# Head-wise top-1 routing: the routing logits move into the experts' matmuls, and half of the masking moves to GpSimd

## The chip, the cores and the metric

The kernel runs on one core of one Trainium2 chip. The metric is the device time of one launch in microseconds (us): 1763.26 us is the median of two runs of the kernel before (1754.2 and 1772.32 us). All data are float32.

## What is computed

```
route_logits = x @ route_w                       # x: 64 x 1024 tokens of 1024, route_w: 1024 x 16
best_head    = argmax(route_logits, axis=-1)     # one of 16 heads per token
x_heads      = x.reshape(B, S, 16, 64)
for h in range(16):
    out[:, :, h, :] = (x_heads[:, :, h, :] @ experts[h]) * (best_head == h)[:, :, None]
```

There are 65536 tokens, 512 tiles of 128 tokens. All sixteen 64x64 products are formed for every token, and all but one head of a token's output are then set to zero by the mask. 268 MB are read and 268 MB written.

## The kernel before, in words

A tile is 128 tokens on the 128 partitions by 1024 columns (512 KB). Four tiles make a group; `for g in range(NG + 1)` goes over 128 groups, and inside it `for t in range(T)` over a group's four tiles. The loop is software-pipelined by one group: while group g is transposed, group g-1 goes through the experts.

Per tile, TensorE makes eight 128x128 transposes (line 99) into the PSUM tile `ps_t`, four to a bank, and ScalarE copies each half to the SBUF tile `xt` (line 102), so that the contraction index lies on the partitions. `expert_tile` then issues 32 small matmuls (line 141): the array is used as four 64x64 tiles, `half` choosing the upper or lower 64 partitions (an even or an odd head) and `th` the upper or lower 64 tokens. Here `xt` is the stationary operand and the expert's 64x64 matrix in `ew` the moving one. VectorE evacuates all 1024 columns of `ps_e` with one multiplication by the mask (line 146) into `ot`.

Once per group, `route` computes the logits separately: eight matmuls with `route_w` stationary and 512 tokens moving (line 111), a ScalarE copy (line 115), four transposes back (line 118), a VectorE reduction over four column groups (line 120) and five small VectorE instructions on 128x64 elements that make the mask (lines 124 to 132).

In the trace every float32 matmul of the code is two MATMUL instructions, each with a weight load (LDWEIGHTS) of its own: 32 in the code are 64 and 64 there. Transposes are one and one. Loads of `x` (line 88) and stores of the output (line 163) are both issued on SyncE's queue, SP, in program order. Twenty `xin` buffers let the loads run 20 tiles ahead: a load waits until the transposes of the tile 20 before it are done. A store waits for the masking of its tile. The order on each engine follows the program.

## Time and profile before

| | |
|---|---|
| median of the two runs | 1763.26 us |
| the profiled execution | 1754.08 us, its span 1752.3 us |
| mean granted TensorE clock | 0.962 |
| busy share of the span | TensorE matmuls 87%, weight loads 65%, VectorE 47%, ScalarE 36%, GpSimd 0% |
| DMA queue of loads and stores | 536.94 MB, 86.8% of 16 engines' time |
| DMA queue of instructions | 310 packets, 5.08 MB, 1.2% |
| median time to landing | load 5.8 us, store 6.5 us |

The shares are of the whole span. A line of the costliest groups gives busy time and mean length of one instruction, and behind the second bar the idle time of the engine before such instructions with what ended it. Matmuls overlap in the array, so the mean length of one is not the distance from one to the next; that distance is read from the timeline. "Issue" is time in which an engine waited for nothing that the profile shows.

### The profile page before, as it was taken

The numbers are of one execution on the slowest core, as the hardware profiler recorded it, in microseconds if no ns is written. First come the engines' busy times: TensorE is split into PE (matmuls) and PEld (weight loads), VectorE is DVE, ScalarE is ACT, GpSimd is POOL, SyncE is SP. The second block draws the span as 40 slices with busy tenths as digits, with TensorE's granted clock in tenths as the row PEclk, the third lists the DMA queues.
The fourth block names the chain that finished last, engine by engine and source line by source line (L and its number), as shares of the span: only waits on it lengthen the run. The fifth ranks groups of instructions, "written<-read, shape, count | busy, mean of one in ns | idle before, by whom it ended". The sixth has DMA issues, their size and how long they took to land.

```text
span 1752.3 us, 84634 instructions
## 1 busy us (share of the span) xinstructions
PE 1517.8 (87%) x39424; PEld 1132.8 (65%) x39424; DVE 824.7 (47%) x1282; ACT 638.2 (36%) x1153; POOL 0.8 (0%) x7
## 2 busy tenths in 40 slices
PE   7888889888889988988889898888888888888898
PEld 5666666666666666666666676666666666665666
DVE  2444444444445544444444454445444444454455
ACT  3333333333333333333333333333333333333343
POOL 0000000000000000000000000000000000000000
PEclk8999999999999999899999999999999999999999
DMA  8999888998889989898998888989998889998864
GB/s 307 379 347 321 297 309 305 320 329 301 306 293 325 328 293 327 283 326 313 315 318 299 315 307 300 312 303 336 312 321 307 313 312 322 314 319 297 300 262 195
DMA packets 149903, 542.68 MB, mean 310 GB/s; under 512 B 18480, under 2 KB 18480, under 8 KB 149552
## 3 DMA queue, kind: packets, MB, share of 16 engines
q1 hardware_dynamic: 147456, 536.94, 86.8%
q8 instruction: 310, 5.08, 1.2%
q10 hardware_dynamic: 2096, 0.33, 0.1%
q14 instruction: 41, 0.34, 0.1%
HBM read 268.76 MB, written 268.44 MB: 307 GB/s over the span
## 4 chain that ended last, share of the span: by engine, by line
PE 86%; issue 12%; DMA 1%; DVE 0%; ACT 0%; ACTq 0%
PE ps_e L141 35%; PE ps_t L99 31%; PE ps_r L111 15%; PE ps_l L118 4%; DMA ew<-in_experts_dram 1%; DVE ot L146 0%; ACT lgt L115 0%; ACTq L70 0%; ACT xt L102 0%; ACTq L115 0%
## 5 line engine op out<-in xcount | busy, mean ns | idle before, releaser
L146 DVE TENSOR_TENSOR ot<-ps_e,mask 128x1024 f32<-128x1024 f32 x512 | 627.0, 1225 | 556.6 <-PE ps_e L141 543.5
L102 ACT COPY xt<-ps_t 128x512 f32<-128x512 f32 x1024 | 565.2, 588 | 662.8 <-PE ps_t L99 662.2
L141 PE MATMUL ps_e<-ew,xt 64*64 64x64 f32 x32768 | 658.0, 226 | 159.9 <-issue 155.2
L141 PEld LDWEIGHTS ps_e<-ew,xt 64*64 64x64 f32 x32768 | 566.8, 138 | 271.6 <-issue 263.3
L99 PE MATMUL ps_t<-ident,xin 128*128 128x128 f32 x4096 | 604.2, 286 | 42.5 <-issue 36.9
L99 PEld LDWEIGHTS ps_t<-ident,xin 128*128 128x128 f32 x4096 | 458.3, 144 | 186.7 <-issue 159.6
L111 PE MATMUL ps_r<-xt,rw 128*32 128x512 f32 x2048 | 279.2, 642 | 20.8 <-issue 20.8
L115 ACT COPY lgt<-ps_r 128x512 f32<-128x512 f32 x128 | 74.9, 585 | 435.3 <-PE ps_r L111 435.3
L120 DVE TENSOR_REDUCE lg<-ps_l 128x64 f32<-128x256 f32 x128 | 54.4, 425 | 342.5 <-PE ps_l L118 342.5
L111 PEld LDWEIGHTS ps_r<-xt,rw 128*32 128x32 f32 x2048 | 57.1, 114 | 127.2 <-issue 117.3
L118 PE MATMUL ps_l<-ident,lgt 128*128 128x128 f32 x512 | 84.0, 286 | 4.3 <-issue 3.8
L118 PEld LDWEIGHTS ps_l<-ident,lgt 128*128 128x128 f32 x512 | 54.8, 142 | 27.0 <-ACT lgt L115 22.8
L126 DVE TENSOR_TENSOR hit<-lg,mx 128x64 f32<-128x64 f32 x128 | 28.9, 225 | 4.4
L132 DVE TENSOR_TENSOR mask<-hit,top 128x64 f32<-128x64 f32 x128 | 28.8, 225 | 4.4
L128 DVE TENSOR_TENSOR hit<-hit,rank 128x64 f32<-128x64 f32 x128 | 28.8, 225 | 4.4
L124 DVE TENSOR_REDUCE mx<-lg 128x4 f32<-128x64 f32 x128 | 28.2, 220 | 4.4
L130 DVE TENSOR_REDUCE top<-hit 128x4 f32<-128x64 f32 x128 | 28.2, 220 | 4.4
L102 ACT ACT_TABLE_LOAD x1 | 1.3, 1283 | 2.9 <-issue 2.9
L74 DVE MEMSET rw<- 128x256 f32 x1 | 0.3, 272 | 0.9 <-PEq L179 0.9
masks.py:199 POOL TENSOR_SCALAR_AFFINE_SELECT ident<-ident 128x128 f32<-128x128 f32 x1 | 0.3, 292 | 0.0
L82 DVE CAST rank<-rank_i 128x64 f32<-128x64 int32 x1 | 0.3, 264 | 0.1
masks.py:197 POOL MEMSET ident<- 128x128 f32 x1 | 0.2, 204 | 0.3 <-POOLq L179 0.3
(5 smaller groups left out, 0.6 us busy)
## 6 DMA issues: line engine op xcount, KB each, us to landing
xin<-in_x_dram SPq DMA_DIRECT2D x512, 512.0 KB, 5.8
out_dram<-ot SPq DMA_DIRECT2D x512, 512.0 KB, 6.5
ew<-in_experts_dram ACTq DMA_DIRECT2D x2, 128.0 KB, 7.7
rw<-in_route_w_dram ACTq DMA_DIRECT2D x1, 64.0 KB, 11.8
```

Of the source, the lines that this page charges most:

```text
L99: nc.tensor.transpose(ps_t[c * w:(c + 1) * w, q, :], xin[:, p * P + c * w:p * P + (c + 1) * w], ident)
L102: nc.scalar.copy(out=xt[:, half * (NB // 2):(half + 1) * (NB // 2), t * P:(t + 1) * P], in_=ps_t)
L111: nc.tensor.matmul(ps_r[c * CW:(c + 1) * CW, :], lhsT=rw[:, p, :], rhs=xt[:, p, :], start=(r == 0), stop=(r == NB // CG - 1))
L115: nc.scalar.copy(out=lgt, in_=ps_r)
L118: nc.tensor.transpose(ps_l[:, t, :], lgt[:, t * P:(t + 1) * P], ident)
L120: nc.vector.tensor_reduce(out=lg, in_=ps_l.rearrange("k t (c h) -> k t h c", c=CG)[:, :, 0:H, :], op=ALU.add, axis=AX.X)
L124: nc.vector.reduce_max(out=mx, in_=lg, axis=AX.X)
L126: nc.vector.tensor_tensor(out=hit, in0=lg, in1=mx.unsqueeze(2).to_broadcast([P, T, H]), op=ALU.is_ge)
L128: nc.vector.tensor_tensor(out=hit, in0=hit, in1=rank, op=ALU.mult)
L132: nc.vector.tensor_tensor(out=mask, in0=hit, in1=top.unsqueeze(2).to_broadcast([P, T, H]), op=ALU.is_equal)
L141: nc.tensor.matmul(ps_e[th * 64:(th + 1) * 64, half, p, :], lhsT=xt[half * 64:(half + 1) * 64, p, t * P + th * 64:t * P + (th + 1) * 64], ...
L146: nc.vector.tensor_tensor(out=ot.rearrange("k (p two e) -> k two p e", two=2, e=Dh), in0=ps_e, in1=mask[:, t, :].rearrange("k (p two) -> k ...
```

## The change

`route`, its ScalarE copy and its transposes go. The moving operand of every expert matmul becomes 80 columns of a new constant `mv`: the 64 columns of the expert and, beside them, the 16 columns of `route_w` for the same 64 input features. For even blocks the logits' columns come last and for odd blocks first, so that two neighbouring blocks overlap in PSUM columns 64 to 79 of a 256-column slot and their logits add up there; `start` is set on every fourth block alone, at the start of a PSUM bank.

The output of a tile is split by `half` into two PSUM tiles of two banks each: `ps_a` (even heads, two buffers) and `ps_b` (odd heads, one buffer). With the two banks of `ps_t` all eight banks are used. VectorE reduces the logits of both, adds them, and finds the arg-max with `max` and `max_index`; the mask is a comparison with a constant row of head numbers. VectorE multiplies the even heads straight out of `ps_a`. ScalarE copies the odd heads from `ps_b` to the SBUF tile `raw`, and GpSimd multiplies them. The copy waits for a count of VectorE, the one that the tile's second reduction gives.

Groups of four are gone: the loop goes over single tiles, with the transposes of tile j issued ahead of the experts of tile j-1. `xt` has three buffers of one tile in place of two of four tiles, and `ot` ten in place of twelve. A store now waits for VectorE and GpSimd.

```diff
+    W = Dh + H
+    mv = consts.tile([P, NB, W], FP32, name="mv")
...
-    def route(xt):
-        ps_r = ps_r_pool.tile([P, G], FP32, name="ps_r", tag="ps_r")
-        for r in range(NB // CG):
-            for c in range(CG):
-                p = r * CG + c
-                nc.tensor.matmul(
-                    ps_r[c * CW:(c + 1) * CW, :], lhsT=rw[:, p, :], rhs=xt[:, p, :],
-                    start=(r == 0), stop=(r == NB // CG - 1))
-        lgt = small.tile([P, G], FP32, name="lgt", tag="lgt")
-        nc.scalar.copy(out=lgt, in_=ps_r)
...
+    def windows(ps):
+        return ps[:, :, 0:2 * W].rearrange("k q (ab w) -> k q ab w", ab=2)[:, :, :, 0:Dh]
...
+        ps_a = ps_a_pool.tile([P, NB // 2, HB // 2], FP32, name="ps_a", tag="ps_a")
+        ps_b = ps_b_pool.tile([P, NB // 2, HB // 2], FP32, name="ps_b", tag="ps_b")
         for p in range(NB):
-            for half in range(2):
+            q, ab = divmod(p, 2)
+            o0 = ab * Dh
+            for half, ps in ((0, ps_a), (1, ps_b)):
                 for th in range(2):
                     nc.tensor.matmul(
-                        ps_e[th * 64:(th + 1) * 64, half, p, :],
+                        ps[th * 64:(th + 1) * 64, q, o0:o0 + W],
...
-                        rhs=ew[half * 64:(half + 1) * 64, p, :],
-                        start=True, stop=True)
+                        rhs=mv[half * 64:(half + 1) * 64, p, :],
+                        start=(p % 4 == 0), stop=(p % 4 == 3), skip_group_check=True)
+        for half, ps in ((0, ps_a), (1, ps_b)):
+            nc.vector.tensor_reduce(
+                out=lg2[:, half, :], in_=ps[:, :, Dh:W].rearrange("k q h -> k h q"),
+                op=ALU.add, axis=AX.X)
+        nc.scalar.copy(out=raw, in_=windows(ps_b))
+        nc.vector.tensor_add(out=lg, in0=lg2[:, 0, :], in1=lg2[:, 1, :])
+        nc.vector.max(out=mx, in_=lg)
+        nc.vector.max_index(out=ix, in_max=mx, in_values=lg)
+        nc.vector.tensor_scalar(
+            out=mask, in0=hid, scalar1=ix[:, 0:1], scalar2=None, op0=ALU.is_equal)
+        nc.vector.tensor_tensor(out=ov[:, 0], in0=windows(ps_a), in1=bc(0), op=ALU.mult)
+        nc.gpsimd.tensor_tensor(out=ov[:, 1], in0=raw, in1=bc(1), op=ALU.mult)
+        nc.sync.dma_start(out=og[j], in_=ot)
```

TensorE's order before, from the experts of a group's last tile to the next group's second tile (`ps_e` is the experts' output, `ps_r` and `ps_l` the logits, x32 means 32 matmuls of the code in a row):

```order
L141 MATMUL ps_e<-ew,xt 64x64 x32
L111 MATMUL ps_r<-xt,rw 32x512 x8
L99 MATMUL ps_t<-ident,xin 128x128 x6
L118 MATMUL ps_l<-ident,lgt 128x128 x4
L99 MATMUL ps_t<-ident,xin 128x128 x2
L141 MATMUL ps_e<-ew,xt 64x64 x32
L99 MATMUL ps_t<-ident,xin 128x128 x8
```

TensorE's order now, from the transposes of one tile into the experts of the tile before it, with what each row waits for (`ps_a` waits for VectorE, `ps_b` for ScalarE):

```order
L96 MATMUL ps_t<-ident,xin 128x128 [waits DMAHW0_49,Activation_49]
L96 MATMUL ps_t<-ident,xin 128x128 x3
L96 MATMUL ps_t<-ident,xin 128x128 [waits Activation_49]
L112 MATMUL ps_a<-mv,xt 64x80 [waits DVE_49]
L112 MATMUL ps_a<-mv,xt 64x80
L112 MATMUL ps_b<-mv,xt 64x80 [waits Activation_49]
L112 MATMUL ps_b<-mv,xt 64x80
L112 MATMUL ps_a<-mv,xt 64x80 x2
L112 MATMUL ps_b<-mv,xt 64x80 x2
```

The rows `ps_r` and `ps_l` are gone, and each run of 32 expert matmuls now has a wait for ScalarE at its third matmul.

VectorE's order before, in one group:

```order
L120 TENSOR_REDUCE lg<-ps_l 128x64
L124 TENSOR_REDUCE mx<-lg 128x4
L126 TENSOR_TENSOR hit<-lg,mx 128x64
L128 TENSOR_TENSOR hit<-hit,rank 128x64
L130 TENSOR_REDUCE top<-hit 128x4
L132 TENSOR_TENSOR mask<-hit,top 128x64
L146 TENSOR_TENSOR ot<-ps_e,mask 128x2x8x64 x4
```

And now, in one tile:

```order
L120 TENSOR_REDUCE lg_1086<-ps_a 128x16 [waits PE_49]
L120 TENSOR_REDUCE lg_1086<-ps_b 128x16 [waits PE_49]
L127 TENSOR_TENSOR lg<-lg_1086 128x16 [waits DVE_49]
L129 MAX mx<-lg 128x8 [waits DVE_49]
L131 MAX_INDEX ix<-mx,lg 128x8 [waits DVE_49]
L133 TENSOR_SCALAR mask<-hid,ix 128x16 [waits DVE_49,Pool_49]
L143 TENSOR_TENSOR ot<-ps_a,mask 128x8x64 [waits DMAHW2_49,DVE_49]
```

Ten instructions for four tiles became seven for each tile; the large product has half the columns, and each of the five from L127 on waits for the one before it.

## Rows read from the trace of the kernel before

**Rows 1.** The page: span, busy time (share) x instructions, and the chain's shares.

```profile
span 1752.3 us, 84634 instructions
PE 1517.8 (87%) x39424; PEld 1132.8 (65%) x39424; DVE 824.7 (47%) x1282; ACT 638.2 (36%) x1153; POOL 0.8 (0%) x7
...
PE 86%; issue 12%; DMA 1%; DVE 0%; ACT 0%; ACTq 0%
```

**Rows 2.** The page's costliest groups: TensorE, the experts' matmuls and their weight loads.

```profile
L141 PE MATMUL ps_e<-ew,xt 64*64 64x64 f32 x32768 | 658.0, 226 | 159.9 <-issue 155.2
L141 PEld LDWEIGHTS ps_e<-ew,xt 64*64 64x64 f32 x32768 | 566.8, 138 | 271.6 <-issue 263.3
```

**Rows 3.** Timeline, TensorE: start us, us, what, [idle before <-releaser].

```profile
807.57 1.04 PE L141 MATMUL ps_e<-ew,xt 64*64 64x64 f32 x55 [2.13 <-issue]
...
808.54 1.09 PE L99 MATMUL ps_t<-ident,xin 128*128 128x128 f32 x8
...
809.56 1.16 PE L141 MATMUL ps_e<-ew,xt 64*64 64x64 f32 x64
...
810.65 0.62 PE L111 MATMUL ps_r<-xt,rw 128*32 128x512 f32 x1
...
813.95 1.92 PE L111 MATMUL ps_r<-xt,rw 128*32 128x512 f32 x15 [2.67 <-issue]
```

**Rows 4.** The page's DMA queues: packets, MB, share of 16 engines' span.

```profile
q1 hardware_dynamic: 147456, 536.94, 86.8%
q8 instruction: 310, 5.08, 1.2%
```

**Rows 5.** 20 us stretches: busy us (x instructions) by engine, granted clock, DMA share, GB/s.

```profile
28.00:48.00 20.00, 17.70 (x459) 12.74 (x458) 9.70 (x16) 7.78 (x14) 0.00 (x0) 1.00 1.00 373
540.00:560.00 20.00, 17.88 (x416) 12.24 (x416) 9.78 (x18) 7.17 (x13) 0.00 (x0) 1.00 0.94 352
780.00:800.00 20.00, 18.83 (x480) 13.96 (x481) 10.12 (x13) 8.15 (x15) 0.00 (x0) 1.00 0.95 323
800.00:820.00 20.00, 15.07 (x414) 11.37 (x415) 8.86 (x17) 6.42 (x13) 0.00 (x0) 1.00 0.84 306
1700.00:1720.00 20.00, 20.00 (x549) 15.10 (x547) 11.46 (x20) 8.83 (x16) 0.00 (x0) 1.00 0.53 213
```

**Rows 6.** Waits in the whole span: us in total, times, longest us.

```profile
PE ps_t L99 <- DMA xin<-in_x_dram: 4.5, 2, 4.4
```

**Rows 7.** Timeline, TensorE and one ScalarE copy, from one route to the second tile's experts.

```profile
1654.51 1.92 PE L111 MATMUL ps_r<-xt,rw 128*32 128x512 f32 x16
...
1656.36 0.87 PE L99 MATMUL ps_t<-ident,xin 128*128 128x128 f32 x6
1656.55 0.58 ACT L115 COPY lgt<-ps_r 128x512 f32<-128x512 f32 x1 [2.39 <-PE ps_r L111]
...
1657.19 0.42 PEld L118 LDWEIGHTS ps_l<-ident,lgt 128*128 128x128 f32 x4 [0.19 <-ACT lgt L115]
...
1658.00 1.16 PE L141 MATMUL ps_e<-ew,xt 64*64 64x64 f32 x64
...
1659.09 1.09 PE L99 MATMUL ps_t<-ident,xin 128*128 128x128 f32 x8
...
1660.11 1.16 PE L141 MATMUL ps_e<-ew,xt 64*64 64x64 f32 x64
```

**Rows 8.** The page's costliest groups: VectorE, ScalarE and GpSimd.

```profile
L146 DVE TENSOR_TENSOR ot<-ps_e,mask 128x1024 f32<-128x1024 f32 x512 | 627.0, 1225 | 556.6 <-PE ps_e L141 543.5
L102 ACT COPY xt<-ps_t 128x512 f32<-128x512 f32 x1024 | 565.2, 588 | 662.8 <-PE ps_t L99 662.2
...
L120 DVE TENSOR_REDUCE lg<-ps_l 128x64 f32<-128x256 f32 x128 | 54.4, 425 | 342.5 <-PE ps_l L118 342.5
...
L126 DVE TENSOR_TENSOR hit<-lg,mx 128x64 f32<-128x64 f32 x128 | 28.9, 225 | 4.4
...
masks.py:199 POOL TENSOR_SCALAR_AFFINE_SELECT ident<-ident 128x128 f32<-128x128 f32 x1 | 0.3, 292 | 0.0
```

## The prediction

> **What bounds the kernel now.** I read the page's shares first, then the chain, the DMA queues, and last the timeline. TensorE is busy for 87% and the chain of the work that ended last runs through it for 86%, with 12% "issue", time in which it waited for nothing that the profile shows [rows 1]. VectorE (47%) and ScalarE (36%) are far from a limit. So the kernel looks TensorE-bound, but the 12% (some 210 us) need a name. They stand at the weight loads and matmuls, above all the experts': 263.3 and 155.2 us [rows 2].

> [...]

> The data are not late yet: TensorE waited for loads twice, 4.5 us [rows 6]. But 88.0% of 1752.3 is 1542 us of DMA work that the change does not touch. With some 25 us at the two ends (estimate from the first load's and the last store's landing, 5.8 and 6.5 us in the table, and a tile's work between) the **floor is about 1567 us**.

> **The change, part by part.**

> *TensorE loses the route.* Per group, 16 instructions `ps_r` take 1656.36 - 1654.51 = 1.85 us, and `ps_l` with the break in the transposes around it 0.6 us (from the six transposes at 1656.36 to the experts at 1658.00 is 1.64 us against 1.02 for a plain set of eight) [rows 7]. That is 2.45 us x 128 = 314 us of TensorE time.

> *The expert matmuls grow from 64 to 80 columns.* 64 of them take 1659.09 - 1658.00 = 1.09 us now [rows 7]. If columns set the time it becomes 1.36, if the number of instructions does, 1.09. I take 1.34, near the first: `ps_r` passes 512 columns in 1.85/16 = 0.116 us, so columns cost there, and 16 more at that rate times 64 are 0.23 us. Cost 0.25 x 512 = 128 us (0 to 138). Transposes stay at 1.02 us.

> *TensorE's tile* is then 1.02 + 1.34 = 2.36 us, against (549 per 20 us, 308 a group) 2.81 before. Unhindered that would be 1208 us, below the DMA floor.

> *A new ring.* `ps_b` has one buffer. Experts end, VectorE makes two reductions, ScalarE copies, and only then may the next tile's `ps_b` be written. The 256- and 1024-element rows, 425 and 1225 ns [rows 8], put VectorE's cost at 158 ns plus 1.04 per element, so a 64-element reduction is 225 ns, as the 64-element product shows. A hand-over takes 0.06 us (the copy that ends at 1656.55 + 0.58 releases a weight load at 1657.19), and the experts' last matmul ends 0.07 us behind the start of the transposes (1658.00 + 1.16 against 1659.09) [rows 7]. The copy is therefore done 0.07 + 3 x 0.06 + 0.45 + 0.59 = 1.29 us behind that start, where the transposes take 1.02. So about 0.27 us a tile are added: 2.63 us, 1347 us in all. Still under the floor, and covered as long as the code is later than that.

> *VectorE's tile*: two reductions 0.45, sum, max, index and mask on 16 elements 4 x 0.175 (up to one more if the index needs two passes), half product 158 + 533 = 0.69, and seven gaps of 0.03: 2.05 to 2.25 us, 1150 us at most. Hidden behind TensorE. If the ring or the index cost more, VectorE is the next to be late, at 3.1 us a tile. *ScalarE*: three copies of 588 ns instead of two and a quarter, 1.76 us: hidden.

> *GpSimd's product*, 128x512 with two inputs, has no row. Lower end: VectorE's 0.69. Upper end: the nearest GpSimd row does 128x128 in 292 ns [rows 8]; four times that, doubled for the second input, is 2.34 us. I take 1.3, near a plain four times, with both ends below TensorE's tile. [...] It delays the store alone, which has ten buffers.

> *SP*: 512 loads and 512 stores as before, now strictly a load and a store in turn, and a store waits for GpSimd too. A load queued behind it is 20 tiles ahead, some 60 us: covered. *Constants*: six small loads instead of three, with the experts needed after two tiles instead of four: a few us at the start at most, while loads of `x` run.

> *Blocks.* 72 pairs x 512 = 36864 matmuls, with their weight loads 36864 x 2 / 254 = 290 blocks, 20 fewer. **Sum:** at an unchanged 5.65 us a block 290 x 5.65 = 1639 us. TensorE's own work in a block falls from 4.63 us to 127/72 x 2.36 = 4.16 us (4.64 where the ring binds), which lets the pace fall; a DMA that nears saturation keeps it up. In the stretches at DMA shares of 0.94 to 1.00 TensorE passes 459, 416 and 480 matmuls in 20 us, on average 452 [rows 5], so 36864 would take 1631 us at loads like those to come. Between 1567 and 1639 I take **1600 us**, 154 below the profiled 1754.08, which itself is 0.5% below the median of 1763.26.

> **Rivals.**

> 1. *The freed time goes into longer waits for code.* With less TensorE work between them, loads and stores crowd the queue, and every block arrives as late as in the stretch at 800: 414 matmuls in 20 us, 6.13 us a block, 290 x 6.13 = 1779 us: no change. For it: the pace at shares of 0.94 and over (416 to 480) is hardly better than at 0.84 (414). Against: at an equal total time the DMA is no fuller than now while blocks are fewer, so the same 5.65 us must give less than 1754. Point from which it decides: 5.95 us a block.

> [...]

> 3. *Slower: GpSimd's product.* It lies in every tile, and three buffers of `raw` and of the mask tie ScalarE and VectorE to it. [...] It decides from 3.4 us. Against: 3.4 us are half as much again as the upper end above.

> 4. *The change does more than I think*: the DMA runs at the 373 GB/s of the stretch at 28 [rows 5], and 536.94 MB take 1440 us. Against: that stretch is at the start, mostly loads.

> **The numbers.** Forecast (1560 to 1660) 0.62, rival 1 (1728 to 1798) 0.12, rival 2 (1660 to 1728) 0.15, rival 3 0.08, rival 4 (below 1560) 0.03. The range 1560 to 1735 takes in the near edge of rival 1, leaves out the rest of it and rivals 3 and 4, and holds 0.80. Two per cent, about what a measurement of this kernel can tell from no change, are 35 us: faster means below 1728, slower above 1798. Faster 0.80, same 0.12, slower 0.08.

> **What would show it.** The instruction queue with about 290 packets; 36864 matmuls, no `ps_r` and `ps_l`; a block's matmuls at 1.09 to 1.36 us per 64; a DMA share of 0.93 to 0.97; "issue" still the largest wait of TensorE; some waits of `ps_b` for ScalarE's copy near 0.3 us; loads landing later than 5.8 us. The prediction is wrong if GpSimd's product is over 3 us, if VectorE's share passes 85% (rival 2), or if "issue" grows past 25% of the chain at a DMA share below 0.9 (rival 1).

## The result, and the profile after

The changed kernel takes 1639.07 us in the median of two runs (1638.12 and 1640.01), against 1763.26 us before: a ratio of 0.9296, 95% interval 0.9089 to 0.9502. It is faster, inside the forecast range (1560 to 1735) and 39 us above its point of 1600. Ratios leave out executions over 1.5% above the fastest of their kernel: one of the kernel before, and four of ten of the run with more blocks below.

The page of the changed kernel, the lines that answer to [rows 1] and [rows 4]:

```profile
span 1638.2 us, 85016 instructions
...
PE 1352.1 (83%) x36864; PEld 1175.2 (72%) x36864; DVE 964.7 (59%) x4097; ACT 813.3 (50%) x1537; POOL 538.1 (33%) x519
...
q1 hardware_dynamic: 147456, 536.94, 90.9%
q8 instruction: 290, 4.75, 1.1%
...
PE 81%; issue 16%; DMA 1%; ACT 1%; DVE 0%; POOLq 0%; ACTq 0%; DVEq 0%
```

The instruction queue moved 290 packets, as counted ahead. 1638.2 / 290 = 5.65 us a block, and before it was 1752.3 / 310 = 5.65 us. The gain of 114 us in the spans is that of 20 blocks at the old pace, 113 us. TensorE's busy time fell too (1518 to 1352 us), and what was not needed for the blocks came back as "issue": 12% of the chain before, 16% now.

The costliest groups of the changed kernel, answering to [rows 2, 8]:

```profile
L144 POOL TENSOR_TENSOR ot<-raw,mask 128x512 f32<-128x512 f32 x512 | 537.3, 1049 | 1096.0 <-ACT xt L97 833.8
L112 PE MATMUL ps_a<-mv,xt 64*64 64x80 f32 x16384 | 766.6, 241 | 118.1 <-issue 114.1
...
L112 PEld LDWEIGHTS ps_a<-mv,xt 64*64 64x64 f32 x16384 | 653.1, 139 | 225.9 <-issue 150.2
...
L97 ACT COPY xt<-ps_t 128x512 f32<-128x512 f32 x1024 | 558.4, 596 | 61.6 <-PE ps_t L96 59.4
...
L143 DVE TENSOR_TENSOR ot<-ps_a,mask 128x512 f32<-128x512 f32 x512 | 353.9, 691 | 19.3 <-DMA out_dram<-ot 1.1
```

GpSimd's product takes 1.05 us (I took 1.3, between 0.69 and 2.34) and VectorE's half product 0.69 as worked out. VectorE works 964.7 / 512 = 1.88 us a tile.

The timeline of the changed kernel (start us, us, what, [idle before <-releaser]), from the experts of one tile over a border of two blocks to the experts of the next but one:

```profile
800.11 0.35 PE L112 MATMUL ps_a<-mv,xt 64*64 64x80 f32 x4
...
800.61 0.69 DVE L143 TENSOR_TENSOR ot<-ps_a,mask 128x512 f32<-128x512 f32 x1
...
802.54 0.13 PEld L112 LDWEIGHTS ps_a<-mv,xt 64*64 64x64 f32 x1 [0.17 <-DVE mx L129]
...
803.86 0.29 PE L112 MATMUL ps_a<-mv,xt 64*64 64x80 f32 x2 [1.25 <-DVE ot L143]
803.86 0.13 PEld L112 LDWEIGHTS ps_a<-mv,xt 64*64 64x64 f32 x2 [1.19 <-issue]
...
805.12 1.09 PE L96 MATMUL ps_t<-ident,xin 128*128 128x128 f32 x8
...
806.15 0.36 PE L112 MATMUL ps_a<-mv,xt 64*64 64x80 f32 x4
806.30 0.29 PE L112 MATMUL ps_b<-mv,xt 64*64 64x80 f32 x2
```

Two things are to be seen. First, the wait of 1.25 us is put down to a VectorE product, but the weight load at the same instant says "issue" for 1.19 us. The tile was free: `ps_a` has two buffers, and the experts of the tile before had started at 800.11, ahead of VectorE's product of 800.61 on the tile before them. So the next instructions were not there. Second, at 806.15 the experts start with four matmuls into `ps_a` and reach `ps_b` 0.15 us later, where four at the pace behind 803.86 (64 up to 805.12) take 0.08: the new ring costs some 0.07 us.

That the instructions were missing can be read directly, since the trace keeps the time of every DMA packet. Behind the first 40 us TensorE has 184 pauses of over 0.6 us between the starts of two instructions. Every one of them ends 1.1 to 1.7 us (1.39 in the median) after a packet of the instruction queue has ended, and from one to the next TensorE executes some 254 instructions or a multiple of that. From the end of such a pause to the start of the next instruction packet it is 3.2 us in the median, and the packet takes 0.95 us: 3.2 + 0.95 + 1.39 = 5.5 us, near the pace of 5.65 us. TensorE's own work in the block runs inside that time.

Stretches of 20 us of the changed kernel (columns as in [rows 5]):

```profile
540.00:560.00 20.00, 18.72 (x503) 16.32 (x498) 13.17 (x56) 11.14 (x21) 7.35 (x7) 0.91 0.96 353
800.00:820.00 20.00, 15.45 (x387) 13.62 (x389) 9.92 (x44) 8.82 (x18) 5.24 (x5) 0.83 0.81 289
...
1590.00:1610.00 20.00, 20.00 (x599) 17.68 (x592) 15.85 (x68) 12.57 (x25) 9.28 (x9) 1.00 0.57 222
```

With the DMA at 0.57, TensorE is never idle and passes 599 matmuls, 72 x 20 / 599 = 2.40 us a tile; under load it passes 387 to 503. That 2.40 is TensorE's own tile, and 127 matmuls of it are 4.24 us of own work in a block.

### The profile page after: what moved, and what is told of

Read it like the earlier page. It is cut to its first block, busy times and chain, and to the rows that moved or that the text cites. A ratio compares the mean times of both kernels' runs of the same rounds, so it can differ in the third digit from the quotient of the medians.

```text
span 1638.2 us, 85016 instructions
## 1 busy us (share of the span) xinstructions
PE 1352.1 (83%) x36864; PEld 1175.2 (72%) x36864; DVE 964.7 (59%) x4097; ACT 813.3 (50%) x1537; POOL 538.1 (33%) x519
## 3 DMA queue, kind: packets, MB, share of 16 engines
q1 hardware_dynamic: 147456, 536.94, 90.9%
## 4 chain that ended last, share of the span: by engine, by line
PE 81%; issue 16%; DMA 1%; ACT 1%; DVE 0%; POOLq 0%; ACTq 0%; DVEq 0%
PE ps_t L96 34%; PE ps_a L112 27%; PE ps_b L112 20%; DMA out_dram<-ot 1%; ACT xt L97 0%; DMA mv<-in_experts_dram 0%; ACT raw L124 0%; DVE ot L143 0%; ACT L97 0%; POOLq L178 0%; DVE lg L127 0%; ACTq L77 0%; DVE lg_25572 L120 0%; DVE lg_25110 L120 0%; DVE lg_16134 L120 0%
## 5 line engine op out<-in xcount | busy, mean ns | idle before, releaser
L144 POOL TENSOR_TENSOR ot<-raw,mask 128x512 f32<-128x512 f32 x512 | 537.3, 1049 | 1096.0 <-ACT xt L97 833.8
L112 PE MATMUL ps_a<-mv,xt 64*64 64x80 f32 x16384 | 766.6, 241 | 118.1 <-issue 114.1
L112 PE MATMUL ps_b<-mv,xt 64*64 64x80 f32 x16384 | 762.3, 241 | 105.2 <-issue 102.0
L112 PEld LDWEIGHTS ps_a<-mv,xt 64*64 64x64 f32 x16384 | 653.1, 139 | 225.9 <-issue 150.2
L112 PEld LDWEIGHTS ps_b<-mv,xt 64*64 64x64 f32 x16384 | 649.3, 139 | 118.7 <-issue 114.8
L124 ACT COPY raw<-ps_b 128x512 f32<-128x512 f32 x512 | 300.3, 586 | 752.1 <-DVE lg L127 5.8
L143 DVE TENSOR_TENSOR ot<-ps_a,mask 128x512 f32<-128x512 f32 x512 | 353.9, 691 | 19.3 <-DMA out_dram<-ot 1.1
L133 DVE TENSOR_SCALAR mask<-hid,ix 128x16 f32<-128x16 f32 x512 | 119.8, 234 | 57.4 <-DVE ix L131 3.7
L129 DVE MAX8 mx<-lg 128x8 f32<-128x16 f32 x512 | 91.0, 178 | 17.6
L131 DVE FIND_INDEX8 ix<-mx,lg 128x8 uint32<-128x16 f32 x512 | 86.3, 169 | 0.0
```

Source lines behind the costliest of these rows:

```text
L112: nc.tensor.matmul(ps[th * 64:(th + 1) * 64, q, o0:o0 + W], lhsT=xt[half * 64:(half + 1) * 64, p, th * 64:(th + 1) * 64], rhs=mv[half * 64 ...
L124: nc.scalar.copy(out=raw, in_=windows(ps_b))
L129: nc.vector.max(out=mx, in_=lg)
L131: nc.vector.max_index(out=ix, in_max=mx, in_values=lg)
L133: nc.vector.tensor_scalar(out=mask, in0=hid, scalar1=ix[:, 0:1], scalar2=None, op0=ALU.is_equal)
L143: nc.vector.tensor_tensor(out=ov[:, 0], in0=windows(ps_a), in1=bc(0), op=ALU.mult)
```

## Experiments

The theory: TensorE's program arrives in blocks of about 256 instructions over the same DMA engines as the data. While the DMA is busy a block comes every 5.4 to 5.7 us or so, and where TensorE has less own work in a block than that, the time is the number of blocks times that pace; the change gains because it has 20 blocks fewer. The rivals: TensorE's own work sets the time (the change took 2.45/4 = 0.61 us of routing out of a tile and added some 0.3); or the DMA's bytes do.

**Fewer blocks, more TensorE work.** All 128 tokens of a tile become the stationary columns of one matmul.

```diff
-                for th in range(2):
-                    nc.tensor.matmul(
-                        ps[th * 64:(th + 1) * 64, q, o0:o0 + W],
-                        lhsT=xt[half * 64:(half + 1) * 64, p, th * 64:(th + 1) * 64],
+                nc.tensor.matmul(
+                    ps[:, q, o0:o0 + W],
+                    lhsT=xt[half * 64:(half + 1) * 64, p, :],
```

> The changed kernel with all 128 tokens of a tile as the stationary columns of an expert matmul, 16 matmuls of 64 rows x 128 columns a tile in place of 32 of 64 x 64: same output, same moving columns in all, but 16 + 16 + 8 = 40 pairs of weight load and matmul a tile instead of 72, so 161 instruction blocks instead of 290. Block theory (the time is blocks times 5.65 us while the DMA is busy): blocks stop being the limit (161 x 5.65 = 910 us), and the DMA floor is next, 1535 to 1580 us at a DMA share of 0.95 or more, with issue waits under 3% of the chain. Rival, TensorE's work sets the time: two 64x128 tiles side by side stream as many columns as four 64x64 ones, so 1639 us again, and more if the longer weight loads show.

Measured: 1584.77 us, ratio to before 0.8964 (0.8894 to 0.9033). Its page and its costliest weight loads:

```profile
span 1583.2 us, 52248 instructions
...
PE 1569.0 (99%) x20480; PEld 1440.7 (91%) x20480; DVE 964.6 (61%) x4097; ACT 802.7 (51%) x1537; POOL 537.0 (34%) x519
...
q8 instruction: 162, 2.65, 0.7%
...
PE 99%; DMA 1%; issue 0%; POOLq 0%
...
L111 PEld LDWEIGHTS ps_a<-mv,xt 64*128 64x128 f32 x8192 | 954.4, 188 | 87.6 <-issue 42.8
```

162 blocks, no "issue" in the chain, TensorE busy for 99%. Its own tile grew from 2.40 to 1583 / 512 = 3.09 us, since 32 matmuls with 128-column weight loads take longer (3.09 - 1.02 = 2.07 us, with 1.02 for the transposes) than 64 with 64-column ones (2.40 - 1.02 = 1.38 us), and the time fell. So the first rival is out: 0.7 us more work a tile made the kernel 54 us faster. The bound that took over is not the DMA floor, as I expected, but TensorE at 3.09 us, and the time lies 5 us over my range.

**More blocks, little more work.** Four matmuls of four columns each are added in a tile, into PSUM columns that nothing reads.

```diff
+            if ab == 1:
+                th, half = divmod(q, 2)
+                ps = (ps_a, ps_b)[half]
+                nc.tensor.matmul(
+                    ps[th * 64:(th + 1) * 64, q, 160:164],
...
+                    rhs=mv[half * 64:(half + 1) * 64, p, 0:4],
+                    start=False, stop=False, skip_group_check=True)
```

> The changed kernel with four more expert matmuls a tile of four columns each, into PSUM columns that nothing reads: 80 pairs a tile instead of 72, 322 blocks instead of 290, with almost no more array work (8 x 4 columns against 64 x 80). Block theory: 322 x 5.65 = 1819 us, at least 1750. TensorE-work rival: at the pace of small matmuls some 0.1 us a tile, 1639 + 50 = 1690 us at most. DMA rival (the 92% busy DMA sets the time): 1639 us.

Measured: 1754.72 us in the median of ten executions, 1748.46 us in that of the six that the ratio to before counts, 0.9877 (0.9815 to 0.9939).

```profile
PE 1439.6 (83%) x40960; PEld 1303.2 (75%) x40960; DVE 967.7 (55%) x4097; ACT 812.0 (47%) x1537; POOL 537.3 (31%) x519
...
q8 instruction: 322, 5.28, 1.3%
...
PE 81%; issue 16%; DMA 1%; DVE 1%; ACT 0%; ACTq 0%; POOLq 0%; DVEq 0%
```

32 blocks more cost 109 us on the medians and gave back nearly the whole gain. The pace is 1744.7 / 322 = 5.42 us, so 1819 was too high. The DMA share is 88.3% here against 92.0%; whether that is why blocks come sooner was not tested. The DMA rival (1639) is out. The TensorE rival was priced too low: TensorE's busy time rose by 88 us, not by 50, which puts that rival at 1727, only a little below the lowest of the six executions (1729.82). So this run alone hardly tells the two apart; the wide version above and the run without routing below do.

**A quarter of the bytes, then half, left out.**

```diff
-        nc.sync.dma_start(out=og[j], in_=ot)
+        nc.sync.dma_start(out=og[j][:, 0:D // 2], in_=ot[:, 0:D // 2])
```

> The changed kernel storing only the first 512 of 1024 output columns of each tile: a quarter of the DMA bytes is left out, every other instruction stays. Block theory: the blocks come sooner when the DMA is less busy; at DMA shares of 0.55 TensorE passes a block in 4.24 us, so between 290 x 4.3 and 290 x 5.1, 1250 to 1480 us, with issue waits below 10%. TensorE-work rival: 1639 us, unchanged. DMA rival: about three quarters, 1230 us, at a share that stays above 0.9.

Measured: 1507.03 us in two runs, above the 1480 that I gave as the upper end, with 12% issue where I had said below 10%; 1511.8 / 290 = 5.21 us a block. The queue of this run suggests why the step is small:

```profile
q1 hardware_dynamic: 147456, 402.72, 81.3%
```

As many packets as before, of fewer bytes on average, and the DMA still busy for 82.6% with the instructions. So the second experiment keeps the packets' size and leaves stores out:

```diff
-        nc.sync.dma_start(out=og[j], in_=ot)
+        if j >= NT - 10:
+            nc.sync.dma_start(out=og[j], in_=ot)
```

> The changed kernel storing only the last 10 of 512 tiles: half of the DMA bytes is left out, in packets of the same size; TensorE's program and its 290 blocks stay. Block theory: with the DMA near half busy a block comes before it is needed, as in the changed kernel's last stretch at a share of 0.57, where 599 matmuls pass in 20 us (2.40 us a tile): 512 x 2.40 + 25 = 1255 us, up to 1330, with issue waits under 8%. TensorE-work rival: 1639 us, unchanged. DMA rival: half of 1510 us of DMA work is no limit any more, so the same as the block theory; this run tells both from the first rival, and shows how far the wait for blocks goes with the DMA.

Measured: 1337.95 us in two runs, 1335.5 / 290 = 4.61 us a block.

```profile
PE 1255.6 (94%) x36864; PEld 1102.9 (83%) x36864; DVE 964.2 (72%) x4097; ACT 805.1 (60%) x1537; POOL 537.5 (40%) x519
...
q1 hardware_dynamic: 75168, 273.71, 61.3%
q8 instruction: 290, 4.75, 1.4%
...
PE 93%; issue 5%; DVE 0%; ACT 0%; DMA 0%; POOLq 0%; ACTq 0%; DVEq 0%
```

The same program, the same 290 blocks, 301 us less, and TensorE back near its own 4.24 us a block. The wait for code went with the DMA's load: 16% issue at a share of 92%, 5% at 63%. Of the pauses over 0.6 us 53 are left behind the first 40 us, and from the end of one to the start of the next instruction packet it is 1.2 us in the median in place of 3.2. That rules out the TensorE rival; the rival of the DMA's bytes would say the same here and is answered by the last experiments. The time lies 8 us over my range: at a share of 63% some blocks are still late (5% issue).

**The routing left out of the kernel before.** The mask is a constant, so the output is not that of the problem; 64 columns, no GpSimd work, and the changed kernel's number of matmuls.

```diff
+    fixed = consts.tile([P, T, H], FP32, name="fixed")
+    nc.vector.memset(fixed, 1.0)
     def route(xt):
-        ps_r = ps_r_pool.tile([P, G], FP32, name="ps_r", tag="ps_r")
...
-        return mask
+        return fixed
```

> The kernel before without its routing: the mask is a constant of ones, so ps_r, ps_l, the copy and the mask's instructions are left out; the expert matmuls keep 64 columns and there is no GpSimd work. It has the changed kernel's 36864 matmuls and 290 blocks, with 0.25 to 0.3 us less TensorE work in a tile. Block theory: 290 x 5.65 = 1639 us, the same as the changed kernel, within 1.5%. TensorE-work rival: less work, so 0.25 x 512 = 128 us below the changed kernel, 1510, or the DMA floor near 1560 us.

Measured: 1625.29 us, ratio to before 0.9185 (0.9113 to 0.9258), which overlaps the changed kernel's interval.

```profile
PE 1272.3 (78%) x36864; PEld 1104.2 (68%) x36864; DVE 627.4 (38%) x515; ACT 560.7 (34%) x1025; POOL 0.8 (0%) x7
...
q8 instruction: 289, 4.73, 1.1%
...
PE 77%; issue 21%; DMA 1%; DVE 0%; ACTq 0%; ACT 0%
```

The queue moved 289 packets: 1635.2 / 289 = 5.66 us a block. With 80 us less TensorE work than the changed kernel it is 14 us faster, within the intervals, and inside the 1.5% that I gave; the rest is "issue", 21%. The TensorE rival (1510, or near 1560) is out. The wider moving operand, the per-tile arg-max and GpSimd's part therefore cost nothing that can be measured here: the time is that of a kernel with as many instructions and no routing at all.

**The kernel before with fewer blocks and nothing else of the change.** Two of the eight blocks of columns take all 128 tokens at once.

```diff
-                for th in range(2):
+                w = P if p < 2 else 64
+                for th in range(P // w):
                     nc.tensor.matmul(
-                        ps_e[th * 64:(th + 1) * 64, half, p, :],
-                        lhsT=xt[half * 64:(half + 1) * 64, p, t * P + th * 64:t * P + (th + 1) * 64],
+                        ps_e[th * w:(th + 1) * w, half, p, :],
+                        lhsT=xt[half * 64:(half + 1) * 64, p, t * P + th * w:t * P + (th + 1) * w],
```

> The kernel before, all of its routing kept, with only two of eight blocks of columns as 64x128 matmuls: 69 pairs a tile on average instead of 77, 278 instruction blocks instead of 310, and some 0.3 us more TensorE work a tile (two of eight against none in the changed kernel: 2.73 against 2.40 us). Same output, nothing else of the change. Block theory: between 278 x 5.65 = 1571 and 1650 us, some 120 to 190 us below the kernel before, the like of what the whole change gave. TensorE-work rival: slower than before, 1763 + 0.3 x 512 = 1920 us.

Measured: 1681.06 us, ratio to before 0.9483 (0.9411 to 0.9555), above my 1650.

```profile
PE 1616.9 (97%) x35328; PEld 1235.3 (74%) x35328; DVE 824.7 (49%) x1282; ACT 636.3 (38%) x1153; POOL 0.8 (0%) x7
...
q8 instruction: 278, 4.55, 1.1%
...
PE 96%; issue 3%; DMA 1%; DVE 0%; ACTq 0%; ACT 0%; DVEq 0%
```

TensorE is now busy for 97% of 1671.8 us with 3% issue: with more work of its own, the work binds at 3.27 us a tile. The rival's 1920 is out. 32 blocks fewer, with all of the routing kept and more TensorE work, give three quarters of the whole change's gain.

**The masking undone, twice.** First VectorE multiplies the odd heads straight out of `ps_b`:

```diff
-        raw = raw_pool.tile([P, NB // 2, 2, Dh], FP32, name="raw", tag="raw")
-        nc.scalar.copy(out=raw, in_=windows(ps_b))
...
-        nc.gpsimd.tensor_tensor(out=ov[:, 1], in0=raw, in1=bc(1), op=ALU.mult)
+        nc.vector.tensor_tensor(out=ov[:, 1], in0=windows(ps_b), in1=bc(1), op=ALU.mult)
```

> The changed kernel with the masking undone to VectorE alone: no copy to raw, no GpSimd product, VectorE multiplies the odd heads out of ps_b itself. Same 290 blocks. VectorE's tile grows by a 0.69 us product to some 2.7 us and the single ps_b buffer is held until that product ends, so TensorE's tile may reach 2.9 us, 5.1 us a block. Block theory: pace stays at 5.65 us, 1639 us within 2%, with a few more waits for VectorE. TensorE-work and VectorE rival: every added 0.3 us a tile shows, 1639 + 150 = 1790 us.

Measured: 2091.96 us, ratio 1.1785 (1.1724 to 1.1845). Neither theory had this. One tile of its timeline and the start of the next:

```profile
803.29 1.12 PE L112 MATMUL ps_b<-mv,xt 64*64 64x80 f32 x26
...
804.38 0.23 PE L112 MATMUL ps_b<-mv,xt 64*64 64x80 f32 x1
...
804.44 0.51 PE L112 MATMUL ps_a<-mv,xt 64*64 64x80 f32 x10
804.65 0.23 DVE L120 TENSOR_REDUCE lg<-ps_b 128x16 f32<-128x64 f32 x1 [1.51 <-PE ps_b L112]
...
805.34 1.15 PE L96 MATMUL ps_t<-ident,xin 128*128 128x128 f32 x8 [0.39 <-ACT xt L97]
...
806.49 0.68 DVE L142 TENSOR_TENSOR ot<-ps_b,mask 128x512 f32<-128x512 f32 x1
...
807.32 1.12 PE L112 MATMUL ps_b<-mv,xt 64*64 64x80 f32 x26
```

`ps_b` is written from 803.29 to 804.61 and next at 807.32: 1.32 us of writing and 2.71 us in which VectorE works through its whole tile, to 807.17, before the one buffer is free, 4.03 us a tile, and 512 x 4.03 = 2063. I had taken the longer of the two where the ring is their sum. The order of the expert matmuls differs as well in this kernel (26 matmuls into `ps_b` come in one run, where the changed kernel goes to and fro between `ps_a` and `ps_b`), so it does not tell what GpSimd's product itself is worth. The second undoing keeps the copy and moves only the product:

```diff
-        nc.gpsimd.tensor_tensor(out=ov[:, 1], in0=raw, in1=bc(1), op=ALU.mult)
+        nc.vector.tensor_tensor(out=ov[:, 1], in0=raw, in1=bc(1), op=ALU.mult)
```

> The changed kernel with the odd heads' product moved from GpSimd to VectorE, still out of the copy in raw: TensorE's order and blocks stay the same, ps_b is freed by the copy as before, VectorE's tile grows by 0.69 us to some 2.8 us. In the earlier undoing, where VectorE read ps_b itself, the single ps_b buffer was held through VectorE's whole tile and the time was 2092 us. If that ring was the cause, and GpSimd's product itself is worth nothing while blocks bind: 1639 us within 2%, up to 1670. Rival, VectorE's length decides: 512 x 2.8 = 1434 stays below, so only the two reductions that come later would show, near 1750 us.

Measured: 1622.03 us, ratio to before 0.9155 (0.9077 to 0.9232): no slower than the changed kernel, and inside what I gave.

```profile
PE 1367.0 (85%) x36864; PEld 1175.9 (73%) x36864; DVE 1245.6 (77%) x4609; ACT 810.5 (50%) x1537; POOL 0.8 (0%) x7
...
PE 75%; issue 14%; DVE 7%; DMA 3%; ACT 1%; ACTq 0%; DVEq 0%
```

VectorE then works 77% of the span, and TensorE still waits for blocks (14% issue). So GpSimd's product gains nothing here. With the ScalarE copy the time is 1622 us, without it 2092 us; since the order of the matmuls differs too, how much of that is the copy's freeing `ps_b` early is not separated.

**A version that beats both.** Part of the blocks of columns as 64x128, the rest as 64x64 (n is 4, 2 and 3):

```diff
-                for th in range(2):
+                w = P if p < n else 64
+                for th in range(P // w):
                     nc.tensor.matmul(
-                        ps[th * 64:(th + 1) * 64, q, o0:o0 + W],
-                        lhsT=xt[half * 64:(half + 1) * 64, p, th * 64:(th + 1) * 64],
+                        ps[th * w:(th + 1) * w, q, o0:o0 + W],
+                        lhsT=xt[half * 64:(half + 1) * 64, p, th * w:(th + 1) * w],
```

> The changed kernel with the first four of a tile's eight blocks of columns as 64x128 matmuls (all 128 tokens) and the other four as 64x64: 8 x 2 + 16 x 2 + 8 = 56 pairs a tile, 226 instruction blocks, same output. TensorE's own tile lies between 2.4 (all 64x64) and 3.09 us (all 64x128), 2.75 us, 6.2 us a block, over the 5.65 at which blocks come. Block theory: neither blocks (226 x 5.65 = 1277) nor TensorE (512 x 2.75 = 1408) bind, the DMA floor does: 1540 to 1575 us, below the all-wide version's 1585. TensorE-work rival: between 1585 and 1639 us.

> The same with two of eight blocks of columns as 64x128: 64 pairs a tile, 258 instruction blocks, TensorE's own tile 2.57 us, 5.1 us a block. Block theory: 258 x 5.65 = 1458 is under the DMA floor, but a block's own work is shorter than the time at which blocks come, so some stalls stay: 1545 to 1590 us. TensorE-work rival: between the 64x64 version and four of eight, 1610 to 1625 us.

> The changed kernel with three of a tile's eight blocks of columns as 64x128 matmuls: 60 pairs a tile, 242 instruction blocks, same output. Two of eight gave 1494 us with 258 blocks and some stalls left, four of eight 1531 us without stalls and TensorE busy for 99%. Block theory: three of eight lie between them in TensorE's own work, 2.84 us a tile, 6.0 us a block, so hardly a stall is left and 512 x 2.84 + 25 = 1480 us (1465 to 1515). TensorE-work rival: halfway between the two neighbours, 1512 us.

Measured: four of eight 1530.55 us (ratio 0.8626, 0.8584 to 0.8668), two 1494.19 (0.8418, 0.8366 to 0.8471), three 1494.76 (0.8430, 0.8366 to 0.8495). Four of eight were below my range by 9 us, two by 51; three came inside. All three lie below what the TensorE rival gave (1585, 1610 and 1512 at least). Pages of the runs with two and with three, in this order:

```profile
span 1500.1 us, 76824 instructions
...
PE 1449.2 (97%) x32768; PEld 1261.4 (84%) x32768; DVE 963.2 (64%) x4097; ACT 804.1 (54%) x1537; POOL 538.5 (36%) x519
...
q1 hardware_dynamic: 147456, 536.94, 96.0%
q8 instruction: 258, 4.23, 1.1%
...
PE 96%; issue 3%; DMA 0%; DVE 0%; ACT 0%; POOLq 0%; ACTq 0%; DVEq 0%
```

```profile
span 1493.8 us, 72728 instructions
...
PE 1476.2 (99%) x30720; PEld 1298.0 (87%) x30720; DVE 964.8 (65%) x4097; ACT 802.4 (54%) x1537; POOL 538.4 (36%) x519
...
q1 hardware_dynamic: 147456, 536.94, 96.4%
q8 instruction: 242, 3.96, 1.1%
...
PE 99%; issue 1%; DMA 0%; ACT 0%; POOLq 0%; ACTq 0%
```

With three, TensorE is busy for 99% and binds at 1493.8 / 512 = 2.92 us a tile; with two, own work is less and a little waiting for blocks is left (3% issue). A block lasts 1500.1 / 258 = 5.81 us with two and 1493.8 / 242 = 6.17 us with three, so waiting ends at some 6 us of work a block here. The changed kernel's 536.94 MB in 147456 packets pass in 1494 us here, so the DMA's bytes do not set its 1639 us either. 145 us come off the changed kernel by fewer instructions for the same product.

## Why the prediction was right, and which term was mis-sized

*What bounds the kernel: right.* That TensorE was waiting for blocks of its own program was read from the count of packets and the distance between stalls; fewer blocks with more work (1585 us), as many blocks with less work (1625 us) and as many blocks with less DMA (1338 us) all moved the time as that says, and each of the 184 pauses of the changed kernel ends just behind an instruction packet, 1.39 us in the median. In the all-wide kernel a block lasts 1583.2 / 162 = 9.8 us and "issue" is 0%; in the changed kernel a block holds 4.24 us of work, the DMA is 92% busy and "issue" is 16%.

*290 blocks x 5.65 us = 1639 us: right to the microsecond in the median.* That exactness is luck in part: the same sum gave 1819 us for 322 blocks, where the runs gave 1755. I moved away from it, to 1600, for two reasons: TensorE's work in a block falls, and the DMA floor lay at 1567. **The first step failed.** Without the route the work in a block is smaller still (1272 us of TensorE in place of 1352) and the pace is 5.66 us; own work below the time in which a block arrives did not enter the pace here. With the same program, less DMA work does move it: 5.21 us at a share of 83% and 4.61 us at 63% (where own work, 4.24 us, is near), against 5.65 us at 92%. Between 88 and 93% the share does not order the pace: 5.65 us in the kernel before (88%), 5.42 with more blocks (88%), 5.66 without the route (91%) and 5.58 with VectorE's masks (93%). What sets it there is open.

*The DMA floor of 1567 us: too high.* I took the busy time of the DMA, 88.0% or 1542 us, as work that any version must pay. It was 92.0% of 1638.2, 1507 us, in the changed kernel and 97.1% of 1500.1, 1457 us, in the version with two of eight, for the same data packets and bytes; that version ended at 1500.1, below the floor. A busy share is therefore no fixed amount of work. The point of 1600 was taken between this floor and 1639, and the lower end of the range rested on it.

*The terms of TensorE's tile:* own tile 2.40 us, worked out 2.36. *The ring:* 0.07 us in place of 0.27, hidden. *VectorE* 1.88 us busy in place of 2.05 to 2.25 with gaps, *GpSimd* 1.05 in place of 1.3, both hidden as said: moving GpSimd's product back to VectorE cost nothing (1622 us).

*The rivals.* Rival 1, blocks later everywhere: its point was 5.95 us, the pace stayed 5.65. It was near in one way: TensorE's busy time fell by 166 us and the time by 114, the rest went into longer waits for code. Rival 2: VectorE's share is 59%, where over 85% was its sign, and VectorE works 1.88 us a tile, where 3.1 was the length at which it would be late; no run shows a term that would bring the time to the 1660 to 1728 given to it. Rival 3: GpSimd's product is a third of its 3.4 us. Rival 4: loads and stores moved at 331 GB/s.

*Signs that I named and that did not come:* a DMA share of 0.93 to 0.97 (it was 0.92), loads landing later than 5.8 us (5.8 still), and waits of `ps_b` for ScalarE's copy near 0.3 us (no such wait stands among the larger ones).

## What to carry to other kernels

Where an engine with very many short instructions shows idle time put down to "issue", divide its instructions by the packets of the instruction queue and the span by those packets (254 instructions and 5.65 us here): if stalls stand a block apart and own work in a block is shorter than a block's pace (4.24 us here), count instructions and not work. Then make the same product of fewer, larger instructions until own work in a block just exceeds the time in which one arrives; beyond that point the larger work cost again here (1495, 1531 and 1585 us for three, four and eight of eight). The ring through the single buffer `ps_b`, in the kernel without ScalarE's copy, cost the sum of writing it and of all that must happen before it is free, 1.32 + 2.71 = 4.03 us a tile; and the busy share of the DMA before was no floor: 1567 us were worked out from it, and the version with two of eight has a span of 1500.1.

## What the runs showed of the hardware

With the same program the pace of blocks fell from 5.65 us at a DMA share of 92% to 5.21 at 83% and 4.61 at 63%; less TensorE work in a block left it at 5.66. The DMA's own time for the same 147456 data packets was no constant: 1521 us in the kernel before, 1489 in the changed kernel, 1440 in the version with two of eight. The granted clock was 0.909 on average without the route (21% issue), 0.945 in the changed kernel (16%), 0.998 in the all-wide one (0%), where TensorE was busy for 99%. In the changed kernel it stood at half in 47 stretches of 182 us in all and at full in the others; a transpose took 421 ns in the median in the former and 273 ns in the latter. That the slower matmuls lengthen the kernel is not shown, since own work below the pace did not enter it. A matmul with a 128-column weight load takes (3.09 - 1.02)/32 = 65 ns, against (2.40 - 1.02)/64 = 22 ns with a 64-column one and the same moving columns, three times as long for twice the tokens. What decides where in the DMA queues a block waits was not tried.
